# Cross-attention queries of the second token half as seven products of 256-token blocks

## The chip, the cores and the metric

The kernel runs on one core of one Trainium2 chip. Its time is the device time of one execution in microseconds (us), and the median of several runs is used. The core has five engines that run side by side, each with its own instruction queue: TensorE (PE: matmuls, and PEld for its weight loads), VectorE (DVE), ScalarE (ACT), GpSimd (POOL) and SyncE (SP), whose queue issues all transfers here. SBUF is the working memory, PSUM the eight banks that matmuls write to.

## What is computed

One decoder layer on 1024 tokens of width 1024: an mLSTM and a forgetting attention in parallel, an output projection, cross attention into 256 memory tokens, an MLP with squared ReLU, a final norm, all in float32. The change touches the queries of the cross attention:

```python
x = x + jnp.concatenate([ml_out, fx_out], axis=-1) @ w_out[l]
x = x + cross_attention(rmsnorm(x, ln_x[l]), rmsnorm(mem, ln_mem[l]), w_xq[l], w_xkv[l], w_xo[l])

def cross_attention(h, memn, w_q, w_kv, w_o):
    q = (h @ w_q).reshape(B, S, X_HEADS, X_DH)          # 4 heads of 256
    k, v = jnp.split(memn @ w_kv, 2, axis=-1)
    s = jnp.einsum('bqhd,bmhd->bhqm', q, k) * (X_DH ** -0.5)
    p = jax.nn.softmax(s, axis=-1)
    o = jnp.einsum('bhqm,bmhd->bqhd', p, v).reshape(B, S, D)
    return o @ w_o
```

## The kernel before

Activations lie feature-major: 128 partitions hold one block of 128 features, eight blocks (KT) make the width, and the columns are tokens, in two halves of 512 (TH). Every matmul operand is cut into two parts, a rounded one (hi) and the rest (lo): `split` (L131) makes hi by ACT (L134, or L137 with a scale) and lo by DVE (L135, L138). `mm3` (L184) then forms a product by three matmuls (L186 to L188): lo x hi, hi x lo, hi x hi. In the profile all products of the kernel carry these three lines; they are told apart by the tiles that they write.

The stages around the change: the last part of the output projection (L1136) adds three blocks of the mixer's output to sums kept in DRAM. Its `full_sink` (L1119) loads a partial sum x1d, adds to it, stores it again, cuts it (scaled by the gain ln_x) into the tiles h2, and adds its squares (POOL, L226) for the norm. The norm's factor itself is applied later, per token, inside the softmax (rcol, L1175 and L1177).

Then the cross attention runs over the two token halves, and in each over four heads (L1328). `cross_head` (L1151) first makes the head's queries: for each of two output tiles (kk) a weight of 128 x 1024 is loaded (`weight_load`, L172, tag wr, two buffers) and cut (`weight_parts`, tags wh and wl, three buffers each), and `proj` (L258) multiplies its eight 128 x 128 blocks with the eight blocks of h2, 512 tokens wide, into PSUM bank mm or m2. Next come the scores against 256 memory tokens (banks sc), the maximum (L1173), exp (L1177), the sums' reciprocals (L1178), the scaling by them on POOL (L1180), transposes (L1185), and the products with the values (bank ov), cut into oh and ol for the projection w_xo. In the last head of the second half the first two output tiles of w_xo (`first_half`, L1319) are written between softmax and transposes; the rest of w_xo follows (L1341 to L1354), then the MLP, whose first matrix is already multiplied by seven block products in place of eight (`left_up` L1244, `Pair` L1377).

The order on each engine in these stages is not written out by hand. A list scheduler sets it ahead of the run: among the instructions whose inputs its own timing model has ready, the one written first comes first. SP's queue is ordered in the same way. A tile waits for a free buffer of its tag. The tags that matter here: act (7 buffers of 128 x 4096: h2, oh, ol and the MLP's activations), w4 (5 of 128 x 1024: the keys and values kx and vx), wr (2), wh and wl (3), r_f (2, 128 x 512), and PSUM mm 1, m2 1, sc 3, tp 2, ov 1 banks. `sub` (L1222) is one subtraction on DVE or POOL.

Of the kernel before, what the change touches and what calls it, by code (L numbers as in the profile page):

```python
# [17 lines left out]
P = 128  # L18
# [26 lines left out]
def hybrid_layer(ctx: ExitStack, tc: tile.TileContext, a: dict, out: bass.AP):  # L45
# [1068 lines left out]
    banks[:] = ["mm", "tp", "m2", "tp"]  # L1114
    h2 = [(act(), act())]
    x1_accs = [w2("b"), w2("b")]
    mix_done = []

    def full_sink(n, hf, ps):  # L1119
        hi, lo = h2[hf]  # L1120
        t = rotate("p", "d", "e")
        with tc.issue_after(last_raw[0].ins):
            load(t, x1d[hf, :, n])
        v.tensor_tensor(out=t, in0=ps, in1=t, op=ALU.add)
        done = load(x1d[hf, :, n], t)
        split(hi[:, n], lo[:, n], t, vec[:, VEC["ln_x"] + n :][:, 0:1])
        square_sum(x1_accs[hf], t, n == 0, add=g)
        if hf == 1 and n == KT - 3:
            mix_done.append(done)
# [6 lines left out]
    for n0 in (0, 4):  # L1136
        ws = [weights(a["w_out_b"][n0 // 2 + i], 6 * P) for i in range(2)]
        for hf in range(2):
            if len(h2) <= hf:
                h2.append((act(), act()))  # L1140
            for n in range(n0, n0 + 4):
# [8 lines left out]

    def cross_head(hd, hf, oh, ol):  # L1151
        q = []
        for kk in range(2):
            t = [rotate(*tags).bitcast(F32R) for tags in ((("b",), ("c",)), (("p",), ("a", "y")))[kk]]
            for _, _, ps in proj(weights(a["w_xq"][2 * hd + kk]), h2, 1, order=[(hf, 0)], into=ps_tile(("mm", "m2")[kk])):
                split(*t, ps, 1.0 / 16.0)
            q.append(t)
        kx, vx = w4(dt=F32R), w4(dt=F32R)
        with tc.issue_after(mix_done[0].ins):
# [27 lines left out]
        for kk in range(2):  # L1187
            n = 2 * hd + kk
            ov = ov_()
            for m in range(2):  # L1190
                mm3(ov, both(vx_parts, lambda z: z[:, m, kk * P : (kk + 1) * P]), pts[m], m == 0, m == 1)
            split(oh[:, n], ol[:, n], ov)

# [125 lines left out]
    def first_half(n):  # L1319
# [5 lines left out]
        cut_h(c, 0, (n % 4,))  # L1325

    os_ = []
    for hf in range(2):  # L1328
        oh, ol = act(), act()
        for hd in range(XH):  # L1330
            steps = cross_head(hd, hf, oh, ol)
            next(steps)
            if hf and hd == XH - 1:
                for n in range(2):
                    first_half(n)
            for _ in steps:
                pass
            if hd == hf == 0:
                row_second(1)
        os_.append((oh, ol))  # L1340
    for n in range(2, KT):  # L1341
# [363 lines left out]
```

## Time and profile before

| | us |
|---|---|
| three runs: median (lowest to highest) | 1512.23 (1511.61 to 1512.63) |
| the profiled execution, its own time | 1512.88 |
| its span | 1511.1 |
| PE busy | 1496.5 |
| DVE busy | 1100.0 |
| ACT busy | 727.0 |
| POOL busy | 514.6 |

The profile shows one execution. A row of groups reads: line, engine, operation, tile written <- tiles read, shape, count | busy us in all, mean ns of one | idle us of the engine before them, and what ended it. A row of one line gives lowest, median and highest ns, and when the first and the last began. A row in order of time gives the start, the duration, then the instruction, and in brackets the idle time before it. In the table by stage each engine has its busy us and its count of instructions, then the granted PE clock as a share of full speed and the DMA share. Printed matmul durations overlap; the distance between two starts is what one costs. A tile's number is left out of its name, and tiles on the tag act, w4, z4, m2 are called act, w, z, m.

### The profile page before, as it was taken

The numbers are of one execution on the slowest core, as the hardware profiler recorded it, in microseconds if no ns is written. First come the engines' busy times: TensorE is split into PE (matmuls) and PEld (weight loads), VectorE is DVE, ScalarE is ACT, GpSimd is POOL, SyncE is SP. The second block draws the span as 40 slices with busy tenths as digits, with TensorE's granted clock in tenths as the row PEclk, the third lists the DMA queues.
The fourth block names the chain that finished last, engine by engine and source line by source line (L and its number), as shares of the span: only waits on it lengthen the run. The fifth ranks groups of instructions, "written<-read, shape, count | busy, mean of one in ns | idle before, by whom it ended". The sixth has DMA issues, their size and how long they took to land.

```text
span 1511.1 us, 21913 instructions
## 1 busy us (share of the span) xinstructions
PE 1496.5 (99%) x7662; PEld 1258.6 (83%) x7662; DVE 1100.0 (73%) x1743; ACT 727.0 (48%) x1360; POOL 514.6 (34%) x545
## 2 busy tenths in 40 slices
PE   9999999999999999999999999999999999999997
PEld 9988888889899888888888788888888888888887
DVE  7666676665788875944457989999996568787765
ACT  7324343334688764644444457566664621122134
POOL 1003030414365441611110044554545366563312
PEclk9999999999999999999999999999999999999998
DMA  6322333435777877934344447777678777776623
GB/s 243 116 79 96 101 104 123 134 126 152 247 254 260 288 247 247 308 119 128 117 159 148 147 144 283 238 262 245 221 269 294 268 276 278 278 272 251 248 87 112
DMA packets 123122, 300.91 MB, mean 199 GB/s; under 512 B 13682, under 2 KB 28332, under 8 KB 116100
## 3 DMA queue, kind: packets, MB, share of 16 engines
q1 hardware_dynamic: 123012, 299.52, 57.3%
q8 instruction: 60, 0.98, 0.3%
q14 instruction: 50, 0.41, 0.1%
HBM read 200.65 MB, written 98.82 MB: 198 GB/s over the span
## 4 chain that ended last, share of the span: by engine, by line
PE 95%; DMA 2%; DVE 1%; ACT 1%; issue 1%; SPq 0%; POOLq 0%; POOL 0%; DVEq 0%; ACTq 0%
PE tp L186 8%; PE tp L187 8%; PE tp L188 8%; PE sc L186 6%; PE sc L188 6%; PE sc L187 6%; PE m L188 6%; PE m L187 6%; PE m L186 6%; PE mm L186 6%; PE mm L187 6%; PE mm L188 6%; PE ov L801 2%; PE ov L186 2%; PE ov L187 2%; PE ov L188 2%
## 5 line engine op out<-in xcount | busy, mean ns | idle before, releaser
L186 PE MATMUL tp<-act,wl 128*128 128x512 f32 (+1 forms) x440 | 172.6, 392 | 0.7 <-ACT row L1398 0.7
L187 PE MATMUL tp<-act,wh 128*128 128x512 f32 (+1 forms) x440 | 172.1, 391 | 0.0
L188 PE MATMUL tp<-act,wh 128*128 128x512 f32 (+1 forms) x440 | 171.8, 391 | 0.0
L135 DVE TENSOR_TENSOR wl<-wr,wh 128x1024 fp32r<-128x1024 f32 (+2 forms) x95 | 124.4, 1310 | 24.4 <-ACT wh L134 24.1
L134 ACT ACTIVATE wh<-wr 128x1024 fp32r<-128x1024 f32 (+2 forms) x95 | 95.7, 1007 | 87.4 <-PE tp L188 36.1
L188 PE MATMUL mm<-act,wh 128*128 128x512 f32 (+1 forms) x332 | 127.4, 384 | 0.0
L186 PE MATMUL mm<-act,wl 128*128 128x512 f32 (+1 forms) x332 | 127.4, 384 | 0.0
L187 PE MATMUL mm<-act,wh 128*128 128x512 f32 (+1 forms) x332 | 127.1, 383 | 0.0
L188 PE MATMUL m<-act,wh 128*128 128x512 f32 (+1 forms) x308 | 117.6, 382 | 0.0
L187 PE MATMUL m<-act,wh 128*128 128x512 f32 (+1 forms) x308 | 117.6, 382 | 0.0
L186 PE MATMUL m<-act,wl 128*128 128x512 f32 (+1 forms) x308 | 117.5, 381 | 0.0
L186 PEld LDWEIGHTS tp<-act,wl 128*128 128x128 f32 x440 | 82.7, 188 | 19.7 <-ACT row L1398 1.2
L188 PEld LDWEIGHTS tp<-act,wh 128*128 128x128 f32 x440 | 82.7, 188 | 19.0
L187 PEld LDWEIGHTS tp<-act,wh 128*128 128x128 f32 x440 | 82.7, 188 | 18.3
L1469 POOL TENSOR_TENSOR z<-wr 128x256 f32<-128x256 f32 x56 | 51.5, 940 | 133.5 <-DMA wr<-w_ff2q 119.0
L186 PE MATMUL sc<-act,wl 128*128 128x512 f32 (+1 forms) x248 | 96.7, 390 | 0.0
L188 PE MATMUL sc<-act,wh 128*128 128x512 f32 (+1 forms) x248 | 96.7, 390 | 0.0
L187 PE MATMUL sc<-act,wh 128*128 128x512 f32 (+1 forms) x248 | 96.7, 390 | 0.0
L134 ACT ACTIVATE wh<-z 128x1024 fp32r<-128x1024 f32 (+1 forms) x54 | 55.4, 1027 | 80.3 <-POOL z L1469 58.3
L135 DVE TENSOR_TENSOR wl<-z,wh 128x1024 fp32r<-128x1024 f32 (+1 forms) x54 | 79.2, 1466 | 9.2 <-ACT wh L134 9.0
L134 ACT ACTIVATE w<-wr 128x768 fp32r<-128x768 f32 (+2 forms) x31 | 25.5, 824 | 106.7 <-PE tp L186 33.2
L188 PEld LDWEIGHTS mm<-act,wh 128*128 128x128 f32 x332 | 62.4, 188 | 12.7
(719 smaller groups left out, 4281.7 us busy)
## 6 DMA issues: line engine op xcount, KB each, us to landing
act<-right SPq DMA_DIRECT2D x49, 1024.0 KB
right<-w SPq DMA_DIRECT2D x56, 256.0 KB
wr<-w_ff2q SPq DMA_DIRECT2D x28, 512.0 KB
right<-r_d SPq DMA_DIRECT2D x49, 256.0 KB
right<-r_e SPq DMA_DIRECT2D x49, 256.0 KB
act<-fqk SPq DMA_DIRECT2D x48, 256.0 KB
wr<-w_in SPq DMA_DIRECT2D x20, 512.0 KB
wr<-w_ff SPq DMA_DIRECT2D x20, 512.0 KB
```

The costliest lines, as they stand in the source:

```text
L134: s.activation(hi, src, AF.Copy)
L135: return v.tensor_tensor(out=lo, in0=src, in1=hi.bitcast(F32), op=ALU.subtract)
L186: nc.tensor.matmul(ps, w[1], x[0], start=first, stop=False, skip_group_check=more)
L187: nc.tensor.matmul(ps, w[0], x[1], start=False, stop=False, skip_group_check=more)
L188: nc.tensor.matmul(ps, w[0], x[0], start=False, stop=last, skip_group_check=more)
L801: nc.tensor.matmul(self.ov[:, c0:], self.fv[:, self.j], t[:, c0:], start=self.j == 0 and t is self.p[1], stop=self.last and t is self.p[0])
L1469: g.tensor_tensor(out=o, in0=x, in1=y, op=op)
```

## The change

Only the second token half's queries are made in another way. For a head, its weight is taken as a 2 x 2 matrix of blocks (two output tiles by two halves of the contraction), and its right-hand side as a 2 x 2 matrix too (two halves of the contraction by two blocks of 256 tokens). The product of the two is formed by seven block products in place of eight, each over four 128-blocks of the contraction and 256 tokens wide.

- `full_sink` no longer cuts the second half; h2 has only the first.
- The right-hand combinations (`right_side`): after the queries of each head of the first half, two blocks of x1d are loaded again into r_f tiles, scaled on ACT, combined by four POOL subtractions of 256 columns, and cut. They lie in three act tiles; t4's operand is kept in a w4 tile and cut after the last of them.
- The left-hand combinations (`left_query`): a head's two weights are loaded as before, but cut in three groups (two products' operands each) and one piece of 512 in a w4 tile (product 4), with one DVE sum and four POOL operations of 512 columns between. They are called up to five products (X_LEAD) ahead; head 0's first two groups stand in the last head of the first half.
- `query_blocks` runs the products in the order 1, 2, 5, 6, 3, 7, 4. Products 1 and 2 share bank mm, 5 and 3 bank m2, and 6, 7, 4 a bank sc. ACT copies product 1 out (p1), DVE makes the sums (`add`), and each of the four query blocks is cut (`give`).
- `cross_head` is given its queries; oh and ol of the second half are gathered from act tiles that come free.

```diff
@@ -1112,18 +1112,21 @@
     while late:
         late.extend(filter(None, [late.pop(0)()]))
     banks[:] = ["mm", "tp", "m2", "tp"]
-    h2 = [(act(), act())]
+    h2 = act(), act()
     x1_accs = [w2("b"), w2("b")]
     mix_done = []
 
+    def ln_x(n):
+        return vec[:, VEC["ln_x"] + n :][:, 0:1]
+
     def full_sink(n, hf, ps):
-        hi, lo = h2[hf]
         t = rotate("p", "d", "e")
         with tc.issue_after(last_raw[0].ins):
             load(t, x1d[hf, :, n])
         v.tensor_tensor(out=t, in0=ps, in1=t, op=ALU.add)
         done = load(x1d[hf, :, n], t)
-        split(hi[:, n], lo[:, n], t, vec[:, VEC["ln_x"] + n :][:, 0:1])
+        if hf == 0:
+            split(h2[0][:, n], h2[1][:, n], t, ln_x(n))
         square_sum(x1_accs[hf], t, n == 0, add=g)
         if hf == 1 and n == KT - 3:
             mix_done.append(done)
@@ -1136,8 +1139,6 @@
     for n0 in (0, 4):
         ws = [weights(a["w_out_b"][n0 // 2 + i], 6 * P) for i in range(2)]
         for hf in range(2):
-            if len(h2) <= hf:
-                h2.append((act(), act()))
             for n in range(n0, n0 + 4):
                 w = both(ws[n // 2 % 2], lambda t: t.rearrange("p (k c) -> p k c", k=3)[:, :, n % 2 * P : n % 2 * P + P])
                 ps = mm()
@@ -1148,13 +1149,127 @@
                     row_second(0)
 
 
-    def cross_head(hd, hf, oh, ol):
+    X_ORDER = (1, 2, 5, 6, 3, 7, 4)
+    X_RIGHT = {1: "11", 2: "21", 5: "t1", 6: "t2", 3: "22", 7: "t3", 4: "t4"}
+    X_GROUP = {1: 0, 2: 0, 5: 1, 6: 1, 3: 2, 7: 2}
+    R = {}
+
+    def right_room(*names):
+        t = act().rearrange("p a b -> p (a b)").rearrange("p (n q k c) -> p n q k c", n=2, q=2, k=4)
+        for e, c in enumerate(names):
+            R[c] = t[:, e, 0], t[:, e, 1]
+        return t[:, 1]
+
+    def cut_right(c, k, x):
+        split(R[c][0][:, k], R[c][1][:, k], x)
+
+    fourth = []
+
+    def right_side(k):
+        if not fourth:
+            for c in (("11", "21"), ("t1", "t2"), ("22", "t3")):
+                right_room(*c)
+            fourth.append(w4((P, 4, 256)))
+        x, y = w2("f"), w2("f")
+        for t, n in ((x, k), (y, 4 + k)):
+            load(t, x1d[1, :, n])
+            s.activation(t, t, AF.Copy, scale=ln_x(n))
+        x1, x2, y1, y2 = (t[:, e * 256 : e * 256 + 256] for t in (x, y) for e in range(2))
+        cut_right("11", k, x1)
+        cut_right("21", k, y1)
+        cut_right("22", k, y2)
+        sub(x1, x2, x1, g)
+        cut_right("t1", k, x1)
+        sub(x1, y2, x1, g)
+        cut_right("t2", k, x1)
+        sub(x2, y2, x2, g)
+        cut_right("t3", k, x2)
+        sub(fourth[0][:, k], y1, x1, g)
+
+    def q_room(kk):
+        return [rotate(*tags).bitcast(F32R) for tags in ((("b",), ("c",)), (("p",), ("a", "y")))[kk]]
+
+    def query_whole(hd):
         q = []
         for kk in range(2):
-            t = [rotate(*tags).bitcast(F32R) for tags in ((("b",), ("c",)), (("p",), ("a", "y")))[kk]]
-            for _, _, ps in proj(weights(a["w_xq"][2 * hd + kk]), h2, 1, order=[(hf, 0)], into=ps_tile(("mm", "m2")[kk])):
+            t = q_room(kk)
+            for _, _, ps in proj(weights(a["w_xq"][2 * hd + kk]), [h2], 1, order=[(0, 0)], into=ps_tile(("mm", "m2")[kk])):
                 split(*t, ps, 1.0 / 16.0)
             q.append(t)
+        return q
+
+    x_jobs = [(hd, i) for hd in range(XH) for i in X_ORDER]
+    x_first = {}
+    for at, (hd, i) in enumerate(x_jobs):
+        if i in X_GROUP:
+            x_first.setdefault((hd, X_GROUP[i]), at)
+    x_prep = sorted(x_first, key=x_first.get)
+    x_raws, x_cuts = {}, {}
+
+    def left_query(hd, group):
+        if group == 0:
+            x_raws[hd] = [weight_load(a["w_xq"][2 * hd + e]) for e in range(2)]
+        r1, r2 = x_raws[hd]
+        x11, x12, x21, x22 = r1[:, :TH], r1[:, TH:], r2[:, :TH], r2[:, TH:]
+        if group == 0:
+            t = w4(dt=F32R)
+            h22, l22 = t[:, :TH], t[:, TH:]
+            split(h22, l22, x22)
+        hi, lo = (sb(t, [P, 1024], 3, F32R) for t in ("wh", "wl"))
+        split(hi, lo, (r1, r2, r1)[group])
+        if group == 0:
+            x_cuts[hd, 4] = both((h22, l22), lambda t: t.rearrange("p (k c) -> p k c", k=4))
+            v.tensor_tensor(out=x21, in0=x21, in1=x22, op=ALU.add)
+            sub(x22, x21, x11, g)
+            sub(x12, x12, x22, g)
+            sub(x11, h22.bitcast(F32), x22, g)
+            g.tensor_tensor(out=x11, in0=x11, in1=l22.bitcast(F32), op=ALU.add)
+        for e in range(2):
+            x_cuts[hd, ((1, 2), (5, 6), (7, 3))[group][e]] = both((hi, lo), lambda t: t[:, e * TH : e * TH + TH].rearrange("p (k c) -> p k c", k=4))
+
+    def query_blocks(hd):
+        q = [q_room(kk) for kk in range(2)]
+        u, t = w2("f"), w2("f")
+        u12, u22, p1 = u[:, :256], u[:, 256:], t[:, :256]
+        held = {}
+
+        def give(kk, e, x):
+            split(*both(q[kk], lambda t: t[:, e * 256 : e * 256 + 256]), x, 1.0 / 16.0)
+
+        def add(out_, ps, x):
+            v.tensor_tensor(out=out_, in0=ps, in1=x, op=ALU.add)
+
+        for n, i in enumerate(X_ORDER):
+            while x_prep and x_first[x_prep[0]] <= 7 * hd + n + X_LEAD:
+                left_query(*x_prep.pop(0))
+            at_ = {1: "mm", 2: "mm", 5: "m2", 3: "m2", 6: "sc", 7: "sc", 4: "sc"}[i]
+            if i in (1, 5, 6):
+                held[at_] = ps_tile(at_)[:, :256]
+            ps, l, r = held[at_], x_cuts.pop((hd, i)), R[X_RIGHT[i]]
+            for k in range(4):
+                mm3(ps, both(l, lambda t: t[:, k]), both(r, lambda t: t[:, k]), i in (1, 5, 6) and k == 0, k == 3, True)
+            if i == 1:
+                s.activation(p1, ps, AF.Copy)
+            elif i == 2:
+                give(0, 0, ps)
+            elif i == 5:
+                add(u22, ps, p1)
+            elif i == 6:
+                add(u12, ps, p1)
+            elif i == 3:
+                add(u12, ps, u12)
+                give(0, 1, u12)
+            elif i == 7:
+                add(u22, ps, u22)
+                give(1, 1, u22)
+            else:
+                add(p1, ps, p1)
+                give(1, 0, p1)
+        return q
+
+    X_LEAD = 5
+
+    def cross_head(hd, hf, q, oh, ol):
         kx, vx = w4(dt=F32R), w4(dt=F32R)
         with tc.issue_after(mix_done[0].ins):
             load(kx.bitcast(F32), kxd[hd].rearrange("p e k c -> p (e k c)"))
@@ -1189,7 +1304,7 @@
             ov = ov_()
             for m in range(2):
                 mm3(ov, both(vx_parts, lambda z: z[:, m, kk * P : (kk + 1) * P]), pts[m], m == 0, m == 1)
-            split(oh[:, n], ol[:, n], ov)
+            split(oh[n], ol[n], ov)
 
     x2d = dram.tile([P, KT // 2, 2, 2, TH], F32, name="x2d")
     ys, free = [[], []], []
@@ -1324,20 +1439,47 @@
             H[c] = h_tile()
         cut_h(c, 0, (n % 4,))
 
+    class Rows(dict):
+
+        def __getitem__(self, at):
+            return dict.__getitem__(self, at[1] if isinstance(at, tuple) else at)
+
     os_ = []
-    for hf in range(2):
-        oh, ol = act(), act()
-        for hd in range(XH):
-            steps = cross_head(hd, hf, oh, ol)
-            next(steps)
-            if hf and hd == XH - 1:
-                for n in range(2):
-                    first_half(n)
-            for _ in steps:
-                pass
-            if hd == hf == 0:
-                row_second(1)
-        os_.append((oh, ol))
+    whole = act(), act()
+    os_.append([Rows(enumerate(t[:, n] for n in range(KT))) for t in whole])
+    for hd in range(XH):
+        q = query_whole(hd)
+        right_side(hd)
+        if hd == XH - 1:
+            last_room = right_room("t4")
+            for k in range(4):
+                cut_right("t4", k, fourth[0][:, k])
+            for _ in range(2):
+                left_query(*x_prep.pop(0))
+        for _ in cross_head(hd, 0, q, *os_[0]):
+            pass
+        if hd == 0:
+            row_second(1)
+    oh, ol = Rows(), Rows()
+    os_.append([oh, ol])
+    for hd in range(XH):
+        q = query_blocks(hd)
+        if hd == 0:
+            t = act()
+            for n in range(4):
+                oh[n], ol[n] = t[:, n], t[:, 4 + n]
+        elif hd > 1:
+            t = last_room if hd == 2 else right_room("-")
+            t = t.rearrange("p q k c -> p (q k c)").rearrange("p (q n c) -> p q n c", q=2, n=2)
+            for n in range(2):
+                oh[2 * hd + n], ol[2 * hd + n] = t[:, 0, n], t[:, 1, n]
+        steps = cross_head(hd, 1, q, oh, ol)
+        next(steps)
+        if hd == XH - 1:
+            for n in range(2):
+                first_half(n)
+        for _ in steps:
+            pass
     for n in range(2, KT):
         first_half(n)
     H.update({c: h_tile() for c in ("t1", "t2")})
```

## The prediction

> **What bounds the kernel now.** I read the page first: the busy shares and the chain of work that ended last.
>
> ```profile
> span 1511.1 us, 21913 instructions
> PE 1496.5 (99%) x7662; PEld 1258.6 (83%) x7662; DVE 1100.0 (73%) x1743; ACT 727.0 (48%) x1360; POOL 514.6 (34%) x545
> PE 95%; DMA 2%; DVE 1%; ACT 1%; issue 1%; SPq 0%; POOLq 0%; POOL 0%; DVEq 0%; ACTq 0%
> ```
>
> TensorE (PE) is busy for 99% of the span and is 95% of the chain. A busy PE need not be at its peak, so the second view is PE in order of time, to see what one matmul costs in a packed row of them: the distance between starts, not the printed duration, which overlaps its neighbour. The third is a table by stage. The first token half's cross attention runs from about 628 us (its first query product) and takes as long as the second, so I cut at 699.5; the third and fourth rows are the output projections that follow.
>
> ```profile
> core 0: us, PE busy (x) PEld busy (x) DVE busy (x) ACT busy (x) POOL busy (x), PEclk, DMA share, GB/s
> 628.10:699.50 71.40, 71.40 (x377) 60.28 (x376) 36.96 (x58) 29.77 (x61) 16.36 (x19) 1.00 0.50 166
> 699.50:770.90 71.40, 71.40 (x372) 60.23 (x371) 32.93 (x54) 30.25 (x65) 9.30 (x16) 1.00 0.39 123
> 770.90:820.00 49.10, 49.10 (x216) 39.57 (x215) 34.22 (x49) 21.90 (x35) 3.33 (x4) 1.00 0.51 172
> 820.00:872.00 52.00, 51.27 (x224) 41.18 (x224) 47.60 (x72) 23.49 (x35) 0.00 (x0) 1.00 0.42 140
> ```
>
> PE has no gap in either half at full granted clock. VectorE (DVE) is under half used there, ScalarE (ACT) also, GpSimd (POOL) hardly at all. So here time is PE time: what PE no longer does comes off the end, as long as the others keep feeding it.
>
> **What it removes and adds on PE.** Before, a head of the second half makes its queries by 2 x 8 x 3 = 48 matmuls of 512 columns (two output tiles, eight blocks of the contraction, three terms of the split product). After: 7 products x 4 x 3 = 84 matmuls of 256 columns. Their prices:
>
> ```profile
> 634.61 0.39 PE L186 MATMUL m<-act,wl 128*128 128x512 f32 x1
> ...
> 640.20 0.28 PE L186 MATMUL sc<-w,r_c 128*128 128x256 f32 x1
> ...
> 646.28 0.28 PE L186 MATMUL sc<-w,r_a 128*128 128x256 f32 x1
> ...
> 648.41 0.39 PE L188 MATMUL mm<-act,wh 128*128 128x512 f32 x1
> ```
>
> From 634.61 to 640.20 lie 24 matmuls of 512: 0.2329 us each. From 646.28 to 648.41 lie 18 of 256: 0.1183 us each, a little over half. Those 256s are the attention scores; the same form as the new products (weights standing, activations moving) is found in the keys' projection:
>
> ```profile
> 425.10 0.28 PE L186 MATMUL mm<-act,wl 128*128 128x256 f32 x1
> ...
> 426.46 0.60 PE L782 MATMUL tp<-ident,act 128*128 128x128 f32 x4
> ```
>
> Twelve in 1.36 us, 0.113 us each. I take 0.118, the price in this stage, and keep both sides: 0.113 and 0.120. A head goes from 48 x 0.2329 = 11.18 us to 84 x 0.118 = 9.91 us, so four heads save 4 x 1.27 = **5.1 us** (6.8 us at 0.113, 4.4 us at 0.120). This is the whole gain; a seventh fewer products is only 0.3% of the span, because it is done in one small stage.
>
> **Bank turnarounds.** Three PSUM banks carry the seven products. Product 2 is added onto product 1 in the same bank after ACT has copied product 1 out, and product 4 onto 7 after DVE has read it; in the written order nothing of the same head lies between these pairs. What one costs with nothing to fill it:
>
> ```profile
> 654.00 0.39 PE L188 MATMUL m<-act,wh 128*128 128x512 f32 x1
> ...
> 654.43 0.60 ACT L137 ACTIVATE r_p<-m 128x512 fp32r<-128x512 f32 x1 [2.17 <-PE m L188]
> ```
>
> The reader starts 0.04 us after the matmul's modelled end (654.39). For 256 columns: 0.28 of matmul, 0.04, about 0.39 of reading (estimate: 0.60 for 512 columns, less the 0.21 that half of a mostly proportional copy saves) and 0.05 back, less the 0.12 that the next matmul would have come after anyway: 0.64 us. Eight of them are 5.1 us unfilled, nothing if filled. The rows above show the filling: at 640.20 six score matmuls stand between two projections, since nothing in this stage is pinned to the written order. The fill is the previous head's scores (24 x 0.118 = 2.8 us), transposes and value products, and product 5, whose operands are other ones. I take one fifth, **+1.0 us**; ends 0 and 5.1.
>
> **Work put beside PE.** The rows by form that price it, from the second half (699.5 to 770.9 us), then single lines:
>
> ```profile
> L135 DVE TENSOR_TENSOR wl<-wr,wh 128x1024 fp32r<-128x1024 f32 x8 | 10.1, 1261 | 1.7 <-ACT wh L134 1.5
> L1180 POOL TENSOR_SCALAR z<-z,c_rden 128x256 f32<-128x256 f32 x16 | 9.3, 600 | 64.9 <-DVE c_rden L1178 64.9
> L134 ACT ACTIVATE wh<-wr 128x1024 fp32r<-128x1024 f32 x8 | 8.5, 1061 | 0.0
> L138 DVE SCALAR_TENSOR_TENSOR r_c<-mm,r_b 128x512 fp32r<-128x512 f32 x4 | 2.8, 688 | 1.6 <-ACT r_b L137 1.6
> L137 ACT ACTIVATE r_b<-mm 128x512 fp32r<-128x512 f32 x4 | 2.4, 594 | 0.0
> ...
> L138 DVE SCALAR_TENSOR_TENSOR act<-tp,rcol,act x5: 476/483/485, 28.8 to 54.4; 128x256 fp32r<-128x256 f32 x5
> ...
> L1223 POOL TENSOR_TENSOR wr<-wr,wr x14: 1292/1298/1674, 910.9 to 1149.7; 128x512 f32<-128x512 f32 x14
> L1223 DVE TENSOR_TENSOR w<-w,w x6: 683/685/1180, 826.3 to 877.4; 128x512 f32<-128x512 f32 x6
> ...
> L1469 POOL TENSOR_TENSOR z<-wr x56: 724/741/1726, 1161.2 to 1424.5; 128x256 f32<-128x256 f32 x56
> ```
>
> First half: each of four right_side steps adds 2 loads of 256 KB, 2 ACT scalings (1.2), 6 cuts of 256 (ACT 0.39, DVE at most 0.48: 2.3 and 2.9) and 4 POOL subtractions (3.0). Four heads: DVE 36.96 + 11.6 + 1.9 (t4) + 3.9 (two early weight cuts, l22 and a sum) = 54 of 71.4, ACT about 49, POOL 16.36 + 12 + 5.2 = 34. The cover is 71.4 us of PE work; nothing is booked. The eight loads go through SP's queue among the weight and key loads; each waits for an r_f buffer. The eight splits taken out of full_sink relieve DVE just before.
>
> Second half, DVE: 32.93 + 4 more weight cuts (5.0) - 8 query cuts (5.5) + 16 cuts of 256 (7.7) + 20 sums out of PSUM (9.6) + 4 x (l22 and one sum, 1.37) = **55** of the 66.3 us that PE then has. ACT: 30 + 10. POOL: 9.3 + 16 x 1.30 = 30. All are below PE: nothing on the path if the spread is even.
>
> **The weights' chain** is the close call. Both raw weights of a head fill the two wr buffers; their first block gives x11 back only after the POOL sums, and the next head's loads wait behind that. Length:
>
> ```profile
> 634.32 11.78 SPq L174 DMA_DIRECT2D wr<-w_xq  x3
> ...
> 636.85 1.06 ACT L134 ACTIVATE wh<-wr 128x1024 fp32r<-128x1024 f32 x1 [1.44 <-DMA wr<-w_xq]
> ```
>
> A load issued at 634.32 is waited for until 636.85, so at most 2.5 us; two are 5.0. Then l22 0.6 + 0.7, a DVE sum 0.7, four POOL sums 5.2, the last cut 1.1 + 1.3: **14.6 us a head**, where PE has 71.4 / 4 - 1.27 = 16.6. It fits, with 2.0 us a head and, once, the four products (5.7 us) that run before the last group is wanted. I book nothing; the queues' delays are rival D.
>
> **Sum.** The profiled execution took 1512.88 us (span 1511.1): 1512.88 - 5.1 + 1.0 = 1508.8. It was 0.65 us above the median of the three runs (1512.23), so I forecast **1508.1 us**.
>
> **The rivals.**
>
> B: the turnarounds stay open. The order is fixed ahead of the run, so a filler that is late leaves the gap. For it: DVE's queue is to be 83% full, so its reads start late. Against it: PE lost nothing in these 143 us, which have such hand-overs too. Time: 1508.1 + 4.1 = 1512.2.
>
> C: DVE becomes the bound of the second half. For it, a row of the stage before, where POOL squares are summed while DVE cuts:
>
> ```profile
> L138 DVE SCALAR_TENSOR_TENSOR act<-r_e,vec,act x5: 751/1571/1779, 607.9 to 633.0; 128x512 fp32r<-128x512 f32 x5
> L226 POOL TENSOR_TENSOR r_b<-r_c,r_b 128x512 f32<-128x512 f32 x14 | 21.9, 1565 | 30.8 <-DVE act L138 23.0 <-ACT r_c L222 6.0 <-DMA r_p<-x1d 1.4
> ```
>
> The same cut takes 0.75 or 1.78 us. If each of the 16 new POOL sums holds DVE for its 1.30, DVE needs 55 + 20.8 = 75.9 us, 4.5 more than the 71.4 of today: 1512.2 + 4.5 = 1516.7. Against it: only operations with both inputs in SBUF vary so (12 x 1.26 + 8 x 0.68 + 12 x 0.48 = 26 us of the 66), which met by chance cost 0.4 x 20.8 = 8 us and leave DVE at 63.
>
> [...]
>
> D, on the slower side: the weights' chain sets the pace, deciding from 16.6 us a head on. Its place is GpSimd's queue: the four sums stand in order with the softmax scalings (4 x 0.6 a head), which wait for a DVE reciprocal, and POOL is idle 64.9 us for that now. With these 2.4, sums at 1.67 under contention (1.5 more) and 0.6 of queue at each of eight steps (4.8), it is 23.3 us, 6.7 late a head. Three heads follow another: 20.1, less 5.7 once, gives 14.4: 1512.2 - 5.1 + 14.4 = 1521.5. Against it: before, the loads ran well ahead of PE (no PE wait).
>
> E: the change doesn't do what it says, the combinations not being ready in the first half. Every product needs all four of a block's cuts, and the last come in head 3. One such chain (2.5 load, 0.6, 0.9, 3.0, 0.9) is 8 us under that head's 17.9 of PE work; if all of it is late, 1512.2 - 5.1 + 8 = 1515.1.
>
> **Chances.** Forecast 0.56, B 0.14, C 0.09, D 0.18, E 0.03. The forecast's own range is 1505.5 (cheap matmuls, 6.8 less, some filled gaps) to 1510.5 (4.4, with half of the turnarounds). A measurement of this kernel can tell about 0.2% from no change, 3.0 us: faster is below 1509.2, slower above 1515.3. Faster: 0.50 of the forecast and 0.02 of B; same: 0.06, 0.12 of B, 0.02 of C and 0.02 of E; slower: the rest of C and E and all of D. So 0.52, 0.22, 0.26. The range goes from 1505.5 to 1518, leaving out 0.14 of D above and 0.04 below.
>
> **What would show it.** The saving: new matmuls of 256 at 0.113 to 0.120 us from start to start, and the stage's PE count up while its length falls by 5. The turnarounds: PE waits on ACT's copy or DVE's sums. C: DVE near full between the halves, cuts of 1024 at 2 us or more. D: PE waits for the last group's cut, GpSimd waiting for c_rden with sums queued behind it. The forecast is wrong if PE's idle time in the second half passes 2 us, or if the price per 256 columns is over 0.125.

## The result, and the profile after

The changed kernel takes 1517.76 us (median of 6 runs, 1517.42 to 1520.81) against 1512.23 us: 5.5 us slower, ratio 1.004 with a 95% interval of 1.0027 to 1.0053. The forecast was 1508.1 us, so the sign was wrong; the time lies in the range, near its upper end, which had been put at 1518 for the rivals' sake. The profiled execution took 1517.68 us. First the page of the changed kernel:

```profile
span 1516.0 us, 22385 instructions
PE 1494.1 (99%) x7806; PEld 1261.8 (83%) x7806; DVE 1125.0 (74%) x1803; ACT 745.2 (49%) x1408; POOL 549.5 (36%) x577
PE 86%; DMA 5%; DVE 3%; POOL 3%; ACT 2%; issue 1%; SPq 0%; POOLq 0%; DVEq 0%; ACTq 0%
```

PE is busy for 2.4 us less, and the span is 4.9 us longer. PE's share of the chain of work that ended last fell from 95% to 86%; transfers, DVE and POOL took it over. So PE work did go away, and waits took its place. PE in order of time in the second half (changed kernel) confirms the price of the new products:

```profile
722.63 0.28 PE L186 MATMUL sc<-act,wl 128*128 128x256 f32 x1
...
723.88 0.28 PE L188 MATMUL sc<-act,wh 128*128 128x256 f32 x1
```

Eleven steps in 1.25 us, 0.114 each; over all packed pairs of such products in that trace the mean is 0.115. A head's 84 are 9.7 us: with 11.2 before, four heads save some 6 us.

To see where the waits are, I took PE's rows in order of time, and for each stretch summed the distances between starts less the packed price of what was started (0.2333 us for 512 columns, 0.1163 for 256; for a transpose I took 0.0625, an estimate). In fact each further transpose in a row adds 0.11 us (the kernel before: two take 0.38 at 657.97, four 0.60 at 657.29), so a stretch that holds eight more of them reads some 0.4 us higher (the changed kernel has eight more than before from 712 to 772, and nine fewer from 640 to 690); every kernel's sum holds all 64. The rest is time in which PE stood or ran slowly. This is worked out from the rows, and holds one profiled execution each, which was the slowest recorded of its kernel in e4, e8 and e16 and the fastest in e14 and e17 (us; "late" means e1's hold, "first" e11's, explained below):

```
                                  600-640  640-690  690-712  712-772  772-900    sum
before                              0.3      1.7      0.4      1.2      2.1      5.7
changed kernel                      4.1      4.8      0.2      5.3      2.4     16.8
e1  late                            0.4      4.7      5.4      4.5      2.2     17.2
e5  late, subtractions on DVE       0.4      3.7      7.2      4.1      2.1     17.5
e6  late, no sums at all            0.4      1.8      0.6      1.2      2.3      6.3
e7  as e5, z4 weight buffer         0.3      3.2      5.3      3.7      3.2     15.8
e8  no left-hand sums               4.2      6.8      0.8      3.0      2.2     17.0
e10 subtractions on DVE             3.8      5.7      2.3      4.7      2.4     18.9
e17 first                           0.4      2.2      4.6      2.6      2.1     11.9
e11 first, subtractions on DVE      0.4      1.7      1.0      5.3      2.3     10.7
e12 as e11, z4 weight buffer        0.3      1.6      3.7      1.5      2.1      9.2
e14 as e11, no left-hand sums       0.4      1.6      1.3      1.2      3.1      7.6
e15 as e12, softmax scaling on ACT  0.3      1.6      3.3      1.0      2.0      8.3
e16 as e11, softmax scaling on ACT  0.4      1.6      0.9      4.9      2.2     10.0
```

The changed kernel loses 11.1 us more than before: 3.8 at the seam into the cross attention (600 to 640), 3.1 in the first half, 3.9 from the change of halves to 772, and 0.3 later. Less the saving of some 6, that is about the 4.9 us of span.

**The seam.** SP's issue of the first reload and ACT in order of time, then PE, then the table by stage, all of the changed kernel:

```profile
616.62 0.42 SPq L1175 DMA_DIRECT2D r_f<-x1d  x1
...
614.30 0.72 ACT L137 ACTIVATE act<-r_p,vec 128x512 fp32r<-128x512 f32 x1 [0.85 <-DVE r_p L1126]
621.67 0.72 ACT L1176 ACTIVATE r_f<-r_f,vec 128x512 f32<-128x512 f32 x1 [6.64 <-DMA r_f<-x1d]
622.30 0.71 ACT L137 ACTIVATE act<-r_e,vec 128x512 fp32r<-128x512 f32 x1
```

```profile
623.49 0.39 PE L188 MATMUL tp<-w,wh 128*128 128x512 f32 x1
624.45 0.50 PE L186 MATMUL m<-act,wl 128*128 128x512 f32 x1 [0.57 <-DVE r_d L1126]
...
631.69 1.05 PE L234 MATMUL ov<-ones,r_b 128*128 128x1 f32 x8 [0.97 <-POOL r_b L226]
632.61 0.56 PE L187 MATMUL mm<-act,wh 128*128 128x512 f32 x1
...
633.39 0.63 PE L186 MATMUL mm<-act,wl 128*128 128x512 f32 x1
633.82 0.63 PE L187 MATMUL mm<-act,wh 128*128 128x512 f32 x1
```

```profile
628.00:632.60 4.60, 3.63 (x19) 2.53 (x19) 3.71 (x6) 1.36 (x3) 4.52 (x3) 1.00 0.59 199
632.60:636.00 3.40, 3.40 (x11) 2.63 (x11) 1.49 (x1) 2.89 (x5) 3.24 (x4) 0.54 0.85 283
```

L1176 is the first scaling of right_side. It stands in ACT's queue ahead of the cuts and squares of the output projection, and its reload of x1d has not landed: ACT stands for 6.64 us with work queued behind it, 1.6 us before the reload is even issued and 5.0 after. DVE then sums late (PE waits 0.57 for a bank), POOL's sums of squares come late (PE waits 0.97 for them), and after this gap PE runs for 3.4 us at a granted clock of 0.54: starts 0.43 us apart in place of 0.23.

**The first half.** The same wait comes again with five of the seven later reloads. The chain can be followed in ACT's rows and then POOL's:

```profile
657.72 0.72 ACT L1176 ACTIVATE r_f<-r_f,vec 128x512 f32<-128x512 f32 x1 [1.16 <-DMA r_f<-x1d]
658.35 0.40 ACT L134 ACTIVATE act<-r_f 128x256 fp32r<-128x256 f32 x1
658.66 0.55 ACT L1292 ACTIVATE z<-sc,c_mx,rcol 128x256 f32<-128x256 f32 x1
```

```profile
661.86 3.29 POOL L1295 TENSOR_SCALAR z<-z,c_rden 128x256 f32<-128x256 f32 x4 [0.95 <-DVE c_rden L1293]
```

The exps (L1292) stand behind the scaling, POOL's softmax scaling waits for their sums, and the transposes wait for POOL. The waits, who for whom (us in total, times, longest):

```profile
ACT r_f L1176 <- DMA r_f<-x1d: 15.4, 6, 6.6
DVE wr L1222 <- DMA wr<-w_xq: 7.0, 3, 3.1
...
PE tp L1300 <- POOL z L1295: 2.8, 6, 0.9
```

**The second half.** Here it is DVE that stands before a load: L1222 is the weights' first sum, x21 + x22.

```profile
722.88 0.69 DVE L1222 TENSOR_TENSOR wr<-wr 128x512 f32<-128x512 f32 x1 [2.55 <-DMA wr<-w_xq]
...
725.50 0.41 DVE L1240 TENSOR_TENSOR r_f<-m,r_f 128x256 f32<-128x256 f32 x1
```

```profile
725.97 0.38 PE L186 MATMUL m<-act,wl 128*128 128x256 f32 x1 [1.82 <-DVE r_f L1240]
```

L1240 reads product 5 out of its bank, so that product 3 can be added there. Product 5 ends at about 722.80 us, when the load's wait is all but over; but the wait has pushed five DVE operations together, L1222 the first of them, and they stand before L1240 for another 2.6 us. PE stands for 1.82 us. The load was late because it was issued late: its buffer came free with the last cut of the head before.

```profile
717.38 1.22 DVE L135 TENSOR_TENSOR wl<-wr,wh 128x1024 fp32r<-128x1024 f32 x1 [2.40 <-ACT wh L134]
718.63 0.33 SPq L174 DMA_DIRECT2D wr<-w_xq  x1
```

POOL has a smaller part. Its softmax scaling stands behind two of the weights' sums, though the reciprocals that it needs are there by 709.2 us, and the transposes wait for it. At 713 and again at 750 us PE loses some 1.4 us in all by this, by the reckoning of the table.

```profile
710.45 2.28 POOL L1338 TENSOR_TENSOR wr<-w,wr 128x512 f32<-128x512 f32 x1
712.72 2.28 POOL L1295 TENSOR_SCALAR z<-z,c_rden 128x256 f32<-128x256 f32 x4
```

### The profile page after: what moved, and what is told of

Its sections match the earlier page's. It is cut to its first block, busy times and chain, and to the rows that moved or that the text cites. A ratio compares the mean times of both kernels' runs of the same rounds, so it can differ in the third digit from the quotient of the medians.

```text
span 1516.0 us, 22385 instructions
## 1 busy us (share of the span) xinstructions
PE 1494.1 (99%) x7806; PEld 1261.8 (83%) x7806; DVE 1125.0 (74%) x1803; ACT 745.2 (49%) x1408; POOL 549.5 (36%) x577
## 4 chain that ended last, share of the span: by engine, by line
PE 86%; DMA 5%; DVE 3%; POOL 3%; ACT 2%; issue 1%; SPq 0%; POOLq 0%; DVEq 0%; ACTq 0%
PE tp L186 8%; PE tp L187 8%; PE tp L188 8%; PE sc L186 6%; PE sc L188 6%; PE sc L187 6%; PE m L186 5%; PE m L187 5%; PE m L188 5%; PE mm L186 5%; PE mm L188 5%; PE mm L187 5%; PE ov L801 2%; PE tp L782 2%; PE ov L186 2%; PE ov L187 2%
## 5 line engine op out<-in xcount | busy, mean ns | idle before, releaser
L135 DVE TENSOR_TENSOR wl<-wr,wh 128x1024 fp32r<-128x1024 f32 (+2 forms) x99 | 133.1, 1346 | 34.3 <-ACT wh L134 34.1
L134 ACT ACTIVATE wh<-wr 128x1024 fp32r<-128x1024 f32 (+2 forms) x99 | 99.6, 1008 | 91.4 <-PE tp L188 32.0
L188 PE MATMUL mm<-act,wh 128*128 128x512 f32 (+1 forms) x332 | 124.1, 374 | 0.0
L187 PE MATMUL mm<-act,wh 128*128 128x512 f32 (+1 forms) x332 | 123.9, 373 | 0.0
L186 PE MATMUL m<-act,wl 128*128 128x512 f32 (+1 forms) x308 | 114.3, 371 | 3.2 <-DVE r_f L1240 1.8
L187 PE MATMUL m<-act,wh 128*128 128x512 f32 (+1 forms) x308 | 113.6, 369 | 0.0
L188 PE MATMUL m<-act,wh 128*128 128x512 f32 (+1 forms) x308 | 113.5, 369 | 0.0
L186 PE MATMUL sc<-act,wl 128*128 128x512 f32 (+1 forms) x280 | 105.7, 377 | 0.0
L188 PE MATMUL sc<-act,wh 128*128 128x512 f32 (+1 forms) x280 | 105.5, 377 | 0.0
L187 PE MATMUL sc<-act,wh 128*128 128x512 f32 (+1 forms) x280 | 105.5, 377 | 0.0
L134 ACT ACTIVATE w<-wr 128x768 fp32r<-128x768 f32 (+3 forms) x35 | 28.0, 801 | 106.9 <-PE tp L186 32.7
L186 PEld LDWEIGHTS mm<-act,wl 128*128 128x128 f32 x332 | 62.8, 189 | 11.7 <-DVE r_p L1126 0.4
```

The lines of the kernel that those rows point to most:

```text
L134: s.activation(hi, src, AF.Copy)
L135: return v.tensor_tensor(out=lo, in0=src, in1=hi.bitcast(F32), op=ALU.subtract)
L186: nc.tensor.matmul(ps, w[1], x[0], start=first, stop=False, skip_group_check=more)
L187: nc.tensor.matmul(ps, w[0], x[1], start=False, stop=False, skip_group_check=more)
L188: nc.tensor.matmul(ps, w[0], x[0], start=False, stop=last, skip_group_check=more)
```

## Experiments

Each kernel is the changed one with the edit shown. Its ratio is to the kernel before on the same chip.

### e1 to e4: which engine's wait is it?

e1 holds the scalings behind the last query cut of their head (cut_done is the last ACT instruction written so far):

```diff
+        cut_done[:] = [next(i for i in reversed(nc.cur_bb.bb.instructions) if i.engine == mybir.EngineType.Activation)]
...
+            with tc.issue_after(cut_done[0]):
-            s.activation(t, t, AF.Copy, scale=ln_x(n))
+                s.activation(t, t, AF.Copy, scale=ln_x(n))
```

> Each right_side's two scalings on ACT are held behind the last query cut of the same head; nothing else is changed. Theory T1 (ACT stands in its in-order queue before an x1d reload that has not landed, and holds up the work queued behind it): ACT's 6.6 us wait at 615 us and the 8.8 us of five later ones go, with them the seam's loss (about 3.7 us of PE time between 620 and 640 us, half of it at half clock), and most of the 3.1 us that PE loses between 660 and 680: 1511 to 1514 us. Rival R1 (GpSimd's new subtractions hold up its queue, the reloads are harmless): the waits of the transposes for the scaled probabilities stay, 1517 us. Rival R2 (the 256-column products cost more than 0.12 us each): 1517.8 us, unchanged.

Measured: 1519.46 us, 1.0049 (1.0034 to 1.0064). The seam's loss went as T1 said, from 4.1 to 0.4 us, yet the time didn't fall: 5.4 us were lost anew between 690 and 712. ACT's rows of e1 there, and its table by stage:

```profile
700.70 0.42 ACT L134 ACTIVATE act<-r_f 128x256 fp32r<-128x256 f32 x1 [2.53 <-POOL r_f L1341]
701.02 0.55 ACT L1295 ACTIVATE z<-sc,c_mx,rcol 128x256 f32<-128x256 f32 x1
...
703.97 0.39 ACT L1255 ACTIVATE r_f<-mm 128x256 f32<-128x256 f32 x1
```

```profile
701.00:704.42 3.42, 0.89 (x4) 0.49 (x4) 1.55 (x4) 3.42 (x13) 0.47 (x1) 1.00 0.72 283
704.42:707.80 3.38, 3.38 (x17) 2.99 (x18) 3.38 (x7) 2.03 (x4) 3.07 (x4) 0.69 0.02 5
```

In the last head the hold is so late that the right side is made across the change of halves. ACT waits for POOL's subtraction, the exps and the copy of product 1 (L1255) stand behind it, PE gets 0.89 us of work in 3.42 (2.11 us of it in one wait for that copy), and then again a lower clock.

e2 takes the wait for the store away, by reloading other data:

```diff
-            load(t, x1d[1, :, n])
+            load(t, a["x"][:, n, TH:])
```

> The reload reads the layer's input x in place of x1d (so the second half's queries are made of other data): same sizes, same queues, but no wait for the store of x1d. T1: if it is the store just before that makes the first reload late, the seam's 3.7 us go and the later waits (buffers and the DMA queue) stay: 1514 us. If reloads are late for another reason (a loaded DMA queue): 1517 us. R1 and R2: 1517 us or more.

Measured: 1516.84 us, 1.0032 (1.0019 to 1.0045). Of the 4.1 us up to 640 only 1.4 went (2.7 left): the store's wait is at most one part of the lateness. T1's 1514 in this form was missed; the time is nearer to the 1517 of late reloads.

e3 leaves POOL's subtractions out:

```diff
-        sub(x1, x2, x1, g)
...
-        sub(x1, y2, x1, g)
...
-        sub(x2, y2, x2, g)
...
-        sub(fourth[0][:, k], y1, x1, g)
+        s.activation(fourth[0][:, k], y1, AF.Copy)
```

> The right-hand side's four POOL subtractions are left out (three cuts take a block uncombined, the fourth operand is a copy by ACT), so the second half's queries are not the layer's. Loads, scalings and cuts stay. R1: the transposes' waits for POOL go (3.1 us between 660 and 680) and part of the seam's 1 us wait for POOL's square sums: 1513.5 to 1515 us. T1: ACT's waits for the reloads stay and with them nearly all of the loss: 1516.5 to 1518 us.

Measured: 1515.98 us, 1.0029 (1.0019 to 1.0038), between the two theories. The first half's loss fell from 4.8 to 2.2 us, as R1 said; at the seam PE lost 6.4, as T1 said of it. Both hold something up.

e4 moves the weights' first sum from DVE to POOL:

```diff
-            v.tensor_tensor(out=x21, in0=x21, in1=x22, op=ALU.add)
+            g.tensor_tensor(out=x21, in0=x21, in1=x22, op=ALU.add)
```

> In the second half the weights' first sum (x21 + x22) is moved from DVE to POOL, so that DVE no longer stands waiting for a weight load. T2 (DVE's 7.0 us of waits for w_xq hold the sums of products behind them, which gives PE its 1.8 us wait near 726): that wait goes, 1515.5 to 1516.5 us. Rival R3 (the weights' chain is too long in itself, 14.6 us of 16.6 with POOL's part made 0.6 us longer here): the last groups come later still, 1518 to 1520 us.

Measured: 1520.73 us, 1.0053 (1.0038 to 1.0068). T2's time was missed. The wait at 726 went, others came: PE lost as much after 712 us (5.1 against 5.3) and more before. The time is a little above R3's figure, and after 712 us PE now waits 1.8 us for cuts of the weights, as R3 has it; the rest of the loss doesn't show that the chain's length is the reason.

### e5 to e8: the saving, and what takes it back

e5 is e1 with the four subtractions on DVE (`sub(x1, x2, x1)` in place of `sub(x1, x2, x1, g)`, and so on).

> As e1 (scalings held back), and the right-hand side's 16 subtractions on DVE in place of POOL. Theory T3 (work handed from ACT to POOL and back to ACT and DVE in fixed orders is what the first half and its seam with the second lose by; e1 only moved the place): e1's loss between 640 and 710 us (about 7 us more than before) falls to 2 or less, 1512 to 1514 us. Rival R5 (the loss there is late DMA, of reloads, keys and the second half's weights): 1516 to 1519 us.

Measured: 1518.84 us, 1.0048 (1.0033 to 1.0063): R5's time. 7.2 us are lost between 690 and 712, so POOL was not what made e1 bad there. The last head's right side still stretches across the change of halves (PE waits 1.2 us for one of its cuts on ACT). PE then waits 2.5 us for a DVE cut that is queued behind L1222's counterpart, which stands 1.7 us for a weight, and a wait of 1.7 us for a key load comes at 652. So late loads have a part, as R5 said, but not the whole.

e6 is e1 with e3's edit, and without the weights' sums:

```diff
-            v.tensor_tensor(out=x21, in0=x21, in1=x22, op=ALU.add)
-            sub(x22, x21, x11, g)
-            sub(x12, x12, x22, g)
-            sub(x11, h22.bitcast(F32), x22, g)
-            g.tensor_tensor(out=x11, in0=x11, in1=l22.bitcast(F32), op=ALU.add)
```

> As e1, and all combinations are left out, right (four subtractions) and left (five sums), so that the second half's queries are not the layer's; the seven products, the cuts, the sums behind the products and all loads stay. If the saving of 5.1 us on PE is real and only the combinations and the reload's place take it back (T3): 1507 to 1508.5 us. Rival R4 (the seven products themselves cost it: three banks, sums between products, 256 columns): 1511 us or more, with PE waits on the products' own sums in the second half.

Measured: 1507.24 us (1506.9 to 1508.03), 0.9971 (0.996 to 0.9982). The saving is real. Its table by stage:

```profile
600.00:640.00 40.00, 40.00 (x177) 32.42 (x176) 25.00 (x33) 18.37 (x29) 22.10 (x15) 1.00 0.75 256
640.00:700.00 60.00, 59.96 (x347) 51.90 (x346) 35.81 (x77) 40.70 (x99) 7.15 (x15) 1.00 0.48 168
700.00:770.00 70.00, 70.00 (x506) 65.50 (x505) 49.30 (x89) 40.08 (x84) 9.46 (x16) 1.00 0.47 150
```

PE has practically no gap with all reloads, cuts, products, bank turnarounds and sums behind the products in place. R4 falls. e6 lies 12.2 us under e1, from which it differs by the combinations alone. Making them is what takes the saving back, by what it does to the queues and the order, for none of their engines is full: in the changed kernel DVE is busy for 40.3 of the 60 us from 640 to 700, ACT for 34.4 and POOL for 25.9.

e7 is e5 with a head's second raw weight in a z4 buffer:

```diff
-            x_raws[hd] = [weight_load(a["w_xq"][2 * hd + e]) for e in range(2)]
+            second = z4()[:, :1024]
+            x_raws[hd] = [weight_load(a["w_xq"][2 * hd]), second]
+            load(second, a["w_xq"][2 * hd + 1])
```

> As e5, and a head's second raw weight goes to a z4 buffer in place of the second wr buffer, so that the next head's first weight can be loaded while this head's sums still run. R3 (the weights' chain through two wr buffers is what the second half loses by): the second half's loss (4 us more than before in the changed kernel) falls under 1.5 us, and the whole comes to 1508 to 1511 us. Rival (the loss there is hand-overs between engines, not the loads): as e5, within 1 us.

Measured: 1517.78 us, 1.0038 (1.0023 to 1.0053), 1.1 us under e5, and far from R3's time. DVE's waits for w_xq before the first sums fell from 4.0 us to 0.2, yet after 712 us PE loses 3.7 where it lost 4.1: at 746 the transposes now wait for POOL's softmax scaling, 2.1 us, and the scaling waits for DVE's reciprocal.

e8 is the changed kernel without the weights' sums (the diff of e6, alone).

> The changed kernel with the weights' five sums (one on DVE, four on POOL for each head) left out, so that the second half's queries are not the layer's. If these sums are what the second half loses by: PE's extra loss between 700 and 760 us (about 3 to 4 us) goes and the seam's and first half's 6.8 us stay, 1513.5 to 1515 us. If it is the products' own sums: 1517 us or more.

Measured: 1518.08 us, 1.0036 (1.0022 to 1.005), the time of the second expectation, but not its cause: after 712 us PE's loss fell from 5.3 to 3.0 us, and the waits that are left are 1.6 us of transposes waiting for POOL's softmax scaling, not for the products' own sums. The seam stayed (4.2), and the first half lost 2 us more than in the changed kernel, where nothing of it was edited: each edit gives the scheduler another order for the rest.

### e10 to e17: the place, the engine, and both

e11 is e5 with the hold moved to the head's first query cut (`if kk == 0:` ahead of the line that sets cut_done), about 6 us earlier.

> As e5 (subtractions on DVE), but each right_side's scalings are held behind the head's first query cut, about 6 us earlier than in e1 and e5. If e1 and e5 lost between 640 and 710 us because the hold itself was too late (the key load behind the reloads in SP's queue, and in head 3 the right side pushed into the second half's start): that 8 us falls to 3 or less, 1513 to 1515 us. If that seam is bound by something else (late weights, DMA at 300 GB/s): as e5, 1517 to 1519 us.

Measured: 1511.07 us (1509.42 to 1513.49), 0.9997 (0.9988 to 1.0006): 7.8 us less than e5 by this line alone, and 2 us under the lower expectation. At the seam, ACT now stands 0.26 us for a reload where it stood 6.64:

```profile
632.71 0.60 ACT L137 ACTIVATE r_b<-mm 128x512 fp32r<-128x512 f32 x1
633.20 0.72 ACT L1178 ACTIVATE r_f<-r_f,vec 128x512 f32<-128x512 f32 x1
634.18 0.73 ACT L1178 ACTIVATE r_f<-r_f,vec 128x512 f32<-128x512 f32 x1 [0.26 <-DMA r_f<-x1d]
```

e17 is that hold alone, with the subtractions on POOL; e10 the subtractions on DVE alone.

> The changed kernel with the scalings held behind the head's first query cut, and nothing else (the subtractions stay on POOL). If the place of the scalings in ACT's queue is the whole of the first half's loss (T1): within 1.5 us of e11, 1511 to 1512.5 us. If the hand-over to POOL costs as well (T3): 1513 to 1516 us.

> The changed kernel with the 16 subtractions on DVE and nothing else (no hold). T1: ACT still waits for the reloads before the second half's stores, the seam's 3.7 us stay: 1515 to 1518 us. T3: most of the loss goes, 1512 to 1514 us.

Measured: e17 1513.2 us, 1.0006 (0.9997 to 1.0016); e10 1520.06 us, 1.0047 (1.003 to 1.0064).

| median, us | no hold | held behind the first cut |
|---|---|---|
| subtractions on POOL | 1517.76 | 1513.2 |
| subtractions on DVE | 1520.06 | 1511.07 |

The four were not all taken on one chip; the kernel before took 1512.07 to 1512.23 us beside them. The place is worth 4.6 us with POOL's subtractions, 9.0 with DVE's. By the medians the engine is worth 2.1 us where the place is right, though the two intervals overlap; without the hold the two can't be told apart (1517.42 to 1520.81 us and 1518.6 to 1520.45). So T1's cause comes first. It isn't the whole: e17 lies where T3 put it. e10 lies above the time that either theory gave it. What POOL does in e17 is seen on DVE, in order of time:

```profile
688.99 1.27 DVE L206 TENSOR_TENSOR c_t<-c_y 128x4 f32<-128x4 f32 x1 [0.25 <-POOL c_y L204]
690.17 1.02 DVE L135 TENSOR_TENSOR act<-w,act 128x256 fp32r<-128x256 f32 x1
691.12 0.68 DVE L207 SCALAR_TENSOR_TENSOR c_t<-c_t,c_var 128x4 f32<-128x4 f32 x1
...
692.06 0.68 DVE L208 SCALAR_TENSOR_TENSOR rcol<-c_t,c_y 128x4 f32<-128x4 f32 x1
```

L207 and L208 work on four columns and take 0.16 us in e5, where no subtraction runs on POOL; here they take 0.68, beside POOL sums in unbroken order, and a PE instruction that needs rcol waits 2.35 us. That is half of what e17 loses between 690 and 712.

e14 is e11 without the weights' sums.

> e11 with the weights' five sums left out, so that the second half's queries are not the layer's. The difference to e11 (1511.1 us) is what the left-hand sums still cost: if all that is left of the 5.1 us is theirs, 1507 to 1508.5 us (e6, with no sums at all, took 1507.2); if it is the right-hand side's, 1510 us or more.

Measured: 1509.54 us (1507.84 to 1510.35), 0.9981 (0.9972 to 0.999), between the two: 1.5 us under e11 by the medians, while its profile shows PE's loss after 712 us at 1.2, as before the change, in place of 5.3.

e12 is e11 with e7's z4 buffer; e15 is e12 with the second half's softmax scaling on ACT; e16 is e11 with that scaling:

```diff
-            g.tensor_scalar(out=pr[:, i], ...)
+            if hf:
+                s.activation(pr[:, i], pr[:, i], AF.Copy, scale=rden[:, i : i + 1])
+            else:
+                g.tensor_scalar(out=pr[:, i], ...)
```

> As e11, with each head's second raw weight in a z4 buffer. If late weights hold DVE at the seam and in the second half (1.7 to 3.1 us each time): 1 to 3 us less than e11, 1510 to 1513 us. If not: as e11 within 1 us.

> As e12, and in the second half the softmax scaling is done by ACT (4 x 0.4 us a head), so that GpSimd's queue holds the weights' sums alone. If the two kinds of work in one queue hold each other up (the transposes' waits for POOL near 746 us, 2 to 3 us): 1508 to 1511 us, faster than before. If not: as e12, or slower by ACT's added 6 us of work.

> As e15 without the z4 buffer (e11 with the second half's softmax scaling on ACT). Between the two it tells which cause weighs more: queue mixing (then within 1 us of e15) or late weights (then 2 us or more above e15).

Measured: e12 1509.92 us, 0.9985 (0.9975 to 0.9994); e15 1509.63 us, 0.9987 (0.9977 to 0.9996); e16 1508.69 us (1507.58 to 1511.14), 0.9981 (0.9971 to 0.999). All three beat both kernels; their intervals overlap, so by time it is not settled which edit is worth more. The traces tell more than the times. After 712 us e12 and e15, with the second weight in a buffer of its own, lose 1.5 and 1.0 us, where e11 loses 5.3; e16, with ACT's scaling alone, still loses 4.9. There the late weight weighs more. But e12 and e15 lose 3.7 and 3.3 us between 690 and 712, where e11 loses 1.0, and that hides it. e16, the lowest, is 3.4 us under the kernel before and 9.1 under the changed one, with the same products and all combinations made. What is left in its profile is again DVE before a late weight (PE then waits 1.6 us for a cut of L138 on DVE):

```profile
728.80 0.68 DVE L1292 TENSOR_REDUCE c_mx<-sc 128x2 f32<-128x512 f32 x1
733.13 0.69 DVE L1226 TENSOR_TENSOR wr<-wr 128x512 f32<-128x512 f32 x1 [3.65 <-DMA wr<-w_xq]
```

## Why the prediction was wrong

**The saving** was right: 5.1 us forecast, with 0.118 us a matmul taken; 0.115 was measured, and e6 shows 4.7 us of it in the time.

**The bank turnarounds** were booked at 1.0 us; e6 keeps them, and PE loses 0.6 us more in it than before, all causes together. The 0.05 us back to PE in the price of one was an estimate; in the changed kernel L1240 ends at 725.91, and the matmul that waits for it starts at 725.97. Rival B's time falls. Its sign, PE waiting for a bank to be read, does appear: 1.82 us in the changed kernel, 2.11 in e1. Both times the reader stood behind a wait in its own queue.

**The step that failed** is "The cover is 71.4 us of PE work; nothing is booked", of the first half. I compared the engines' busy time with PE's, and by that measure there is room: even in the changed kernel ACT and POOL are far from full. But the cover has to be there at the instruction's place in a fixed queue. I named what the eight loads wait for (an r_f buffer, SP's queue), and not what waits behind the instruction that needs them: on ACT, the cuts and squares of the projection, then the exps. That cost 3.8 us at the seam, with the lower clock, and 3.1 in the first half; e1, e11 and e17 remove the first, e11 and (nearly) e17 the second too. e3, without POOL's subtractions, brings the first half down as well (2.2 us lost), so the hand-over to POOL is part of what cost there. And the combinations were taken as ready "in the first half" in one sum; where a head's part falls in that half mattered more than its size, as e5 against e11 shows.

**The price of a load** was misread as well. "A load issued at 634.32 is waited for until 636.85, so at most 2.5 us" pairs a wait with the wrong issue. The two wr buffers are filled and cut in turn, and the cut at 636.85 is that of the load before (the kernel before, SP's queue):

```profile
628.60 0.40 SPq L174 DMA_DIRECT2D wr<-w_xq  x1
```

That load took 8.2 us. The one issued at 634.32 is waited for by the next cut, until 643.42, so it took 9.1; the DMA engines were 0.93 to 0.99 busy meanwhile. In the changed kernel the first reload took 5.0 us, with them 0.79 busy, and the weight issued at 718.63 took 4.2.

**The second half** was booked at the turnarounds' 1.0 us, and 3.9 were lost; PE stood for 2.7 of the 71.4 us from 699.5 on, over the 2 us that the prediction set as a sign. "It fits, with 2.0 us a head" failed too. With 4.2 us a load, 14.6 becomes 18.0 by the prediction's own sum (an estimate), over the 16.6 that PE had, and the first sums (L1222) of the last three heads in fact start at 703.07, 722.88 and 741.85, 19.8 and 19.0 us apart. PE didn't wait for the last groups' cuts: the chain had begun at 681.1 us, 15 us before the first product. But the chain's first link stands in DVE's queue before a load, with the products' sums behind it: 2.0 us of PE's loss, and POOL's scaling behind the sums is some 1.4.

**Rival D** had the right stage and much of the cause: a chain of over 16.6 us a head, and a queue in order with a waiting instruction in front. It looked for the wait on POOL, which has the smaller part, and its 14.4 us was far too much. e14 shows that the weights' sums bring the loss about, and e12 and e15 that the shared load buffer matters.

**Rival C** (DVE as the bound) falls as put: over the second half DVE is busy for 50.3 of 71.4 us. DVE slower beside POOL is seen in the kernel before, where POOL sums squares (DVE's cuts L138 with all inputs in SBUF took 0.73 to 1.78 us there, its 15 sums L1124 with one input in PSUM 0.67 to 0.69), and in e17 (L207 and L208 at 0.68 us, against 0.16 in e5); it is worth 2.1 us at most in the medians.

**Rival E** is nearest for the first half: the preparation there did fail to stay hidden. I gave it 0.03, since I asked only whether the operands would be ready, and not whom their making would hold up. That the measured time lies in the range is luck: the range reached that far for C and D, at prices that none of the runs bear out.

What stays open: how each order comes about. The waits for DMA at the head of ACT's and DVE's queues suggest that the scheduler's model takes loads to land earlier than they do here; no run shows its times. Between 690 and 712 PE waits in e12 for cuts on DVE (1.1 and 1.3 us); why they come late there is open. And e8 and e10 lose at places that their edits don't touch, so single differences of about 2 us between these kernels can't be put down to the edit alone.

## What to carry to other kernels

Work that is moved beside a bound engine did not stay hidden here where an instruction in front of other work in its queue waited: at the seam ACT stood 6.64 us before a reload in the changed kernel and PE lost 4.1 us from 600 to 640; in e11 it was 0.26 and 0.4. So for each added instruction that needs a transfer, ask what is queued behind it on that engine, and hold it behind an instruction that comes when the data is surely there, but still well ahead of its use. Leaving out the added work whole (as e6) tells in one run whether the saving is real, before its parts are looked at; then change the place before the engine.

## What was not expected of the hardware

After the 0.97 us gap at the seam, PE's granted clock was 0.50 from 632.87 to 636.28 us, 3.41 us long (the row of the table above begins earlier, so its mean is 0.54). Nine matmuls took 3.73 us there from start to start, in place of 2.10, so the price of the gap more than doubles. e1 shows 0.50 for 3.41 us again, from 705.72 on, after its gap of 2.1 us (its row begins earlier, so its mean is 0.69), and e5 for 6.82 us, from 701.56 on, in and after a gap of 2.5 (its rows of 699 to 703, 706.4 and 710 have means of 0.82, 0.50 and 0.72). But the gap of 1.82 us at 726 was followed by full clock (changed kernel, table by stage):

```profile
726.00:729.40 3.40, 3.40 (x25) 3.17 (x26) 3.27 (x7) 3.06 (x6) 2.23 (x5) 1.00 0.00 0
```

At the seam PE stood for 0.97 us, and with the eight matmuls of one column that follow the gap it is 1.9 us, about as long as the gap at 726 that was followed by full clock. Why the clock fell after the one and not after the other can't be told from these runs.
